# Three pairs by token halves instead of four, and twelve seven-block products ahead of the second projection, in layer 0 of a hybrid decoder trunk

## The chip, the cores and the metric

The kernel runs on one core of a Trainium2 chip. Its time is the device time of one execution in microseconds (us); the figure that counts is the median of several executions. A profile is one such execution, recorded by the hardware profiler. PE is TensorE, PEld its weight loads, DVE is VectorE, ACT is ScalarE, POOL is GpSimd, SP is SyncE, which here only issues DMAs.

## The reference

512 tokens of width 1024 go through two layers. Layer 0 is a causal convolution module and a SwiGLU feed-forward network (FFN); layer 1 is sliding-window attention over a shared K/V and a second FFN. The change touches layer 0 alone:

```python
# layer 0
h = h + conformer_conv(rmsnorm(h, norm_mix[0]), ...)   # pointwise + GLU, 31-tap depthwise conv,
                                                       # LayerNorm, swish, second pointwise ("pw2")
h = h + swiglu_ffn(rmsnorm(h, norm_ffn[0]), ffn_w_up[0], ffn_w_down[0])

def swiglu_ffn(x, w_up, w_down):                       # width 1024 -> 2 x 2816 -> 1024
    gate, up = jnp.split(x @ w_up, 2, axis=-1)
    return (jax.nn.silu(gate) * up) @ w_down
```

All values are float32.

## The kernel before

**Arithmetic.** Activations are kept transposed (channels on the 128 partitions, tokens along the row). Most float32 products are done in three passes: `mm3` splits weight and activation into a high and a low part of type float32r and adds high x high, high x low and low x high. Each weight chunk is 128x1024 floats (512 KB). SP loads it into a `raw` tile (six buffers); ACT casts it to `whi`, and DVE subtracts to get `wlo` (four buffers each). This is done three chunks ahead of TensorE (`SPLIT_AHEAD`), in the fixed order `PLAN`. A cast for chunk n can run only when the fourth chunk before it has left its `whi` buffer, that is, when TensorE has finished with it.

**Layer 0 by token halves.** The 512 tokens go through the convolution in two halves of 256 (`h0`, `h1`). The FFN's 2816 hidden channels are eleven pairs of 256. Pairs 0 to 3 (`HALVES0[0]`) are computed for each token half as soon as that half is there: up products, gate, down products. For the first half (`part 0`) each chunk is 24 matmuls with 256 columns (`mm3`; the second projection and pair 0 use unsplit float32); for the second half (`twin`, `mm2`) each chunk is 16 matmuls: high x (high and low side by side), 512 columns, and low x high, 256 columns.

**Layer 0 by seven products.** Pairs 4 to 10 are computed for all 512 tokens with a Winograd form of Strassen's scheme: weights and activations are cut into 2x2 blocks, and seven block products (`SEVEN`: A11, S1, S2, A12, S3, S4, A22, each against a block or a sum of blocks of x) replace eight. Each product is one chunk: 24 matmuls with 256 columns. The sums of weight blocks S1 to S4 are made in DRAM: SP copies a block, POOL issues a DMA that adds another onto it (`prepare`, one step for each `share` of a chunk). The sums of x, T1 to T4 (`Rows0.sums`), are made on DVE as a job that is spread over part 1. The products A12 of pairs 4, 5 and 6 (`FIRST`) need the first token half alone and stand before the second half's projection; ACT copies their results away.

**What sets the order.** `PLAN` sets the order of the chunks. `job(gen, *points)` spreads a generator's steps over the following chunks by hand-written points (chunk count, steps done). The second half's convolution (`second`: taps on DVE, POOL and ACT, then the LayerNorm statistics through TensorE, then the rows `z`) is such a job; a call of `flush` runs what is left. The framework's scheduler then orders each engine's instructions from the program, within what depends on what.

Per seven-product pair DVE and ACT bring the products from PSUM into a tile `c` (c11, c12, c21, c22), then `gates` multiplies by the norm's scale, applies SiLU on ACT, multiplies on POOL, and `split` writes the hidden rows (`hid0`) in high and low parts. After all seven pairs the down products (512 columns, 14 chunks of 24 matmuls) run, and attention follows.

The lines that the prediction speaks of: L380 to L382 are the three matmuls of `mm3`, L412 and L413 the two of `mm2`, L378 unsplit float32; L294 and L297 are the cast and the subtraction of a weight chunk, L261 its load, L289 the accumulating DMA of `prepare`; L1089 is the matmul that spreads the second half's LayerNorm scales, L1101 to L1103 and L544/L545 make the rows `z`; L1295 makes T1 to T4; L830 to L842 bring products from PSUM; L849, L850, L852 and L853 are `gates`. In the changed kernel the same lines stand a little lower (L294 becomes L297, L297 becomes L300, L1103 becomes L1124).

## Time and profile before

| what | value |
|---|---|
| median of three runs | 1044.91 us (1043.2 to 1046.06) |
| profiled execution | 1043.27 us, of which the span from first to last instruction is 1041.5 us |
| busy in the span | PE 1031.5 us, PEld 932.6, DVE 776.5, ACT 613.0, POOL 473.2 |
| granted TensorE clock | 0.997 |
| instructions | 17709 |

A row of a view of groups reads: line, engine, operation, tiles out<-in, shapes, count | busy us in all, mean ns of one | idle us before them and what ended it. A row of the timeline reads: start in us, duration, engine, line, operation, tiles, count. Matmuls overlap in the array, so their durations are longer than their distance from start to start, and it is that distance which adds up to time.

### The profile page before, as it was taken

The page shows a single profiled execution, that of the slowest core. Times are in us where ns is not written, and L with a number is a line of the kernel's source. Part 1 is how long each engine was busy: PE and PEld are TensorE (multiplying, and loading weights), DVE is VectorE, ACT ScalarE, POOL GpSimd, SP SyncE. Part 2 cuts the span into 40 slices and gives each one's busy share as a digit, 9 for nine tenths or more (in the row PEclk, how much of TensorE's full clock was granted, in tenths as well). Part 3 has the DMA queues.
Part 4 walks back from the last instruction along what each step waited for, and adds up shares of the span by engine and source line. Part 5 has one row for each costly group of instructions (what it writes and reads, how often), then busy time and mean ns, then how long its engine had stood idle before and what let it go on. Part 6 is the DMA issues. An engine that isn't in the chain of part 4 may idle for free.

```text
span 1041.5 us, 17709 instructions
## 1 busy us (share of the span) xinstructions
PE 1031.5 (99%) x6580; PEld 932.6 (90%) x6580; DVE 776.5 (75%) x1202; ACT 613.0 (59%) x1062; POOL 473.2 (45%) x569
## 2 busy tenths in 40 slices
PE   9999999999999999999999999999999999999996
PEld 8888889999988999998888877788989999898995
DVE  3999989978789777673536566678686877868777
ACT  3887798847776556552333565466655556554654
POOL 3999999930535233221214255405442334434134
PEclk9999999999999999999999999999999999999998
DMA  9999747999999988999969766955879988877742
GB/s 356 340 315 207 205 126 204 272 256 275 249 239 262 304 220 284 256 301 244 286 209 254 210 183 183 228 154 152 252 230 312 287 264 264 245 233 222 224 150 81
DMA packets 67282, 248.33 MB, mean 238 GB/s; under 512 B 7579, under 2 KB 13884, under 8 KB 66364
## 3 DMA queue, kind: packets, MB, share of 16 engines
q1 hardware_dynamic: 54236, 200.75, 55.9%
q0 software_dynamic: 12672, 46.14, 24.8%
q8 instruction: 51, 0.84, 0.3%
q10 hardware_dynamic: 288, 0.31, 0.1%
q14 instruction: 35, 0.29, 0.1%
HBM read 241.93 MB, written 97.52 MB: 326 GB/s over the span
## 4 chain that ended last, share of the span: by engine, by line
PE 98%; DMA 0%; DVE 0%; issue 0%; POOLq 0%; SPq 0%; POOL 0%; ACT 0%
PE bank L380 20%; PE bank L382 20%; PE bank L381 20%; PE bank L960 10%; PE bank L902 9%; PE bank L412 4%; PE bank L378 4%; PE bank L413 2%; PE bank L1441 1%; PE bank L1483 1%; PE bank L1470 1%; PE bank L1058 1%; PE bank L1607 1%; PE bank L948 1%; DMA both<-in_lead_dram 0%; PE bank L1562 0%
## 5 line engine op out<-in xcount | busy, mean ns | idle before, releaser
L297 DVE TENSOR_TENSOR wlo<-raw,whi 128x1024 fp32r<-128x1024 f32 x246 | 329.7, 1348 | 136.8 <-ACT whi L294 136.5
L294 ACT CAST whi<-raw 128x1024 fp32r<-128x1024 f32 x246 | 257.1, 1049 | 276.6 <-PE bank L381 194.1
L380 PE MATMUL bank<-quad,whi 128*128 128x256 f32 (+1 forms) x976 | 307.4, 317 | 0.0
L381 PE MATMUL bank<-quad,whi 128*128 128x256 f32 (+1 forms) x976 | 306.6, 315 | 0.0
L382 PE MATMUL bank<-quad,wlo 128*128 128x256 f32 (+1 forms) x976 | 305.7, 315 | 0.0
L380 PEld LDWEIGHTS bank<-quad,whi 128*128 128x128 f32 x976 | 185.5, 191 | 12.8 <-issue 1.6
L381 PEld LDWEIGHTS bank<-quad,whi 128*128 128x128 f32 x976 | 186.0, 191 | 11.9 <-issue 0.5
L382 PEld LDWEIGHTS bank<-quad,wlo 128*128 128x128 f32 x976 | 185.6, 191 | 11.8 <-issue 0.4
L853 POOL TENSOR_TENSOR up<-up 128x512 f32<-128x512 f32 x34 | 62.9, 1851 | 283.6 <-ACT up L850 283.6
L1002 POOL TENSOR_TENSOR pr<-pr,pr 128x256 f32<-128x256 f32 x208 | 155.4, 788 | 2.6 <-ACT pr L1001 2.5
L380 PE MATMUL bank<-rows,whi 128*128 128x256 f32 x488 | 138.0, 283 | 0.0
L381 PE MATMUL bank<-rows,whi 128*128 128x256 f32 x488 | 137.8, 282 | 0.0
L382 PE MATMUL bank<-rows,wlo 128*128 128x256 f32 x488 | 137.8, 282 | 0.0
L1009 DVE SCALAR_TENSOR_TENSOR bank<-apad,wdw,bank 128x256 f32<-128x256 f32 x248 | 112.4, 485 | 3.4
L1001 ACT ACTIVATE pr<-apad,wdw 128x256 f32<-128x256 f32 x208 | 98.3, 502 | 14.9 <-POOL pr L1002 13.1
L960 PE MATMUL bank<-quad,w 128*128 128x256 f32 x448 | 98.7, 380 | 0.0
L960 PEld LDWEIGHTS bank<-quad,w 128*128 128x128 f32 x448 | 84.9, 190 | 11.8 <-DVE bank L1009 0.2
L380 PEld LDWEIGHTS bank<-rows,whi 128*128 128x128 f32 x488 | 93.1, 191 | 0.3
L381 PEld LDWEIGHTS bank<-rows,whi 128*128 128x128 f32 x488 | 93.1, 191 | 0.3
L382 PEld LDWEIGHTS bank<-rows,wlo 128*128 128x128 f32 x488 | 93.0, 191 | 0.0
L491 POOL TENSOR_TENSOR tmp<-tmp,tmp 128x256 f32<-128x256 f32 (+1 forms) x28 | 26.8, 957 | 101.4 <-ACT tmp L487 96.2
L412 PE MATMUL bank<-quad,whi 128*128 128x512 f32 x168 | 59.7, 398 | 0.0
(230 smaller groups left out, 1635.9 us busy)
## 6 DMA issues: line engine op xcount, KB each, us to landing
raw<-in_W_dram SPq DMA_DIRECT2D x170, 512.0 KB, 5.7
raw<-sum SPq DMA_DIRECT2D x88, 512.0 KB, 5.4
sum<-in_W_dram SPq DMA_DIRECT2D x52, 512.0 KB, 6.2
sum<-in_W_dram POOLq DMA_DIRECT2D x44, 512.0 KB, 9.6
sum<-sum POOLq DMA_DIRECT2D x44, 512.0 KB, 8.5
sum<-in_W_dram SPq DMA_DIRECT2D x4, 3584.0 KB, 30.4
w<-in_W_dram SPq DMA_DIRECT2D x14, 512.0 KB, 8.6
sum<-in_W_dram SPq DMA_DIRECT2D x4, 1024.0 KB, 30.3
```

The costliest lines, as they stand in the source:

```text
L294: on_act = nc.scalar.copy(hi, src).ins
L297: latest[:] = [on_act, lo_engine[0].tensor_sub(lo, src, f32(hi)).ins]
L380: nc.tensor.matmul(out, w[0], x[0], start=start, stop=False, **kw)
L381: nc.tensor.matmul(out, w[0], x[1], start=False, stop=False, **kw)
L382: nc.tensor.matmul(out, w[1], x[0], start=False, stop=stop, **kw)
L412: nc.tensor.matmul(first[2], first[0], first[1], start=start, stop=False)
L853: pool_op(nc.gpsimd.tensor_mul(gate, gate, c[:, m, :, 1, :]))
L902: nc.tensor.matmul(out, x, w[:, ws], start=first and e == 0 and i == 0, stop=e == 1 and i == 2, skip_group_check=True)
L960: mm = nc.tensor.matmul(self.pb[:, w * W2:(w + 1) * W2], w1_of(ct, w, k), x[k] if x else xg[k][:, tok], start=k == 0, stop=k == KT - 1)
L1001: on_act = nc.scalar.mul(pr, a[:, j:j + W2], tap(j))
L1002: on_pool = pool_op(nc.gpsimd.tensor_add(pr, acc, pr))
L1009: on_dve = nc.vector.scalar_tensor_tensor(yt if i == nd - 1 else c, src, tap(i), c if i else self.shift, op0=ALU.mult, op1=ALU.add)
```

## The change

`HALVES0` puts three pairs instead of four through the token halves, so that eight pairs (3 to 10) go by seven products. Ahead of the second projection stand twelve products instead of three: A12 of all eight pairs and A11 of pairs 4 to 7; where a pair has both, A12 is added onto A11 in the same PSUM bank, and ACT copies both stages away. Part 2 is cut in two groups of four pairs (`GROUPS0`), each followed by its down products. The points of the second convolution's job reach over 50 counts instead of 35; those of the sums of x begin at count 10 instead of 11 and end at 27 instead of 32. The LayerNorm statistics are ordered behind the last matmul issued (`stamp`). The addition of the first half's FFN into `h` is put off into the early products (`let_go`). `share`, the sums of weights prepared for each chunk, is 0.5 instead of 0.45 in the halves and 0.45 instead of 0.25 in part 2. The tiles `c` of odd pairs move to another pool.

```diff
-HALVES0 = ((0, 4), (4, 11))
-FIRST = (4, 5, 6)
+HALVES0 = ((0, 3), (3, 11))
+GROUPS0 = ((3, 7), (7, 11))
+FIRST11 = (4, 5, 6, 7)
+FIRST = [(4, "A11"), (3, "A12"), (4, "A12"), (5, "A11"), (8, "A12"), (5, "A12"),
+         (6, "A11"), (9, "A12"), (6, "A12"), (7, "A11"), (10, "A12"), (7, "A12")]
...
-        if pair in FIRST:
-            names = ["A11", "S1", "S2", "S4", "S3", "A22"]
+        names = ["A11", "S1", "S2", "S4", "S3", "A22"][pair in FIRST11:]
         steps += [(pair, names[0])] + held
-        held = [(pair, names.pop())] if pair in FIRST else []
+        held = [(pair, names.pop())]
...
-    plan.extend(("up0", *step) for step in part2_products())
-    downs(*HALVES0[1])
+    for group in GROUPS0:
+        plan.extend(("up0", *step) for step in part2_products(group))
+        downs(*group)
...
             if a == "A11":
-                if self.early is None:
+                if "A12" in self.early:
+                    nc.vector.tensor_add(c11, r, self.early["A12"])
+                else:
                     nc.scalar.copy(c11, r)
...
+            elif a == "S1" and self.p1 is not None:
+                nc.scalar.copy(c11, self.early["A12"])
+                nc.vector.scalar_tensor_tensor(c22, r, -1.0, self.p1, op0=ALU.mult, op1=ALU.subtract)
             elif a == "S1":
                 nc.scalar.mul(c22, r, -1.0)
+            elif a == "S2" and self.p1 is not None:
+                nc.vector.tensor_add(c12, r, self.p1)
             elif a == "S2":
                 nc.scalar.copy(c12, r)
...
+            elif a == "A22" and self.p1 is not None:
+                nc.vector.scalar_tensor_tensor(c21, r, -1.0, self.p1, op0=ALU.mult, op1=ALU.subtract)
...
-        job(second, (base, 0), (base + 8, 19), (base + 13, 22), (base + 26, 40), (base + 30, 45), (base + 34, 50), (base + 35, h1.n_steps - early - 3))
+        job(second, (base, 0), (base + 8, 17), (base + 13, 20), (base + 26, 34), (base + 38, 40), (base + 41, 43), (base + 42, 44),
+            (base + 43, 44), (base + 44, 45), (base + 45, 46), (base + 47, 48), (base + 48, 49), (base + 50, h1.n_steps - early))
...
-        preparing[0], share[0] = prepare(), 0.45
+        preparing[0], share[0] = prepare(), 0.5
...
-        for pair in FIRST:
+        chains = {}
+        for n, (pair, a) in enumerate(FIRST):
             pace()
-            r = new_chain()
-            product(("up0", pair, "A12"), [[x0["ffn0"][4 + k][e][:, HALF[0]] for k in range(4)] for e in range(2)], r, True)
-            nc.scalar.copy(first[pair], r)
+            if n < 2:
+                let_go()
+            begins = pair not in chains
+            r = chains.setdefault(pair, new_chain() if begins else None)
+            j = 4 * (a == "A12")
+            product(("up0", pair, a), [[x0["ffn0"][j + k][e][:, HALF[0]] for k in range(4)] for e in range(2)], r, begins, pace)
+            nc.scalar.copy(first[pair][a], r)
         flush()
...
-    job(rows0.sums(), (base + 11, 0), (base + 19, 8), (base + 26, 14), (base + 32, 17))
+    job(rows0.sums(), (base + 10, 0), (base + 14, 8), (base + 17, 10), (base + 20, 12), (base + 23, 14), (base + 27, 17))
...
-    share[0] = 1 / 4
+    share[0] = 0.45
+    for group in GROUPS0:
...
         for g in range(2):
             banks = accs(512)
             down_group([(("down", 0, kp, g), 2 * (kp - lo0)) for kp in range(lo0, hi0)], lambda kt: hid0[kt], banks)
             for m in range(4):
                 nc.vector.tensor_add(h[g * 4 + m], banks[m], h[g * 4 + m])
-                nxt.on_h(g * 4 + m)
+                if last:
+                    nxt.on_h(g * 4 + m)
```

ACT, from the LayerNorm scales of the second half (L1085, in the changed kernel L1106) to the first two rows `z` (SiLU at L1103, now L1124, and their cast), before. whi504 belongs to the last early product, whi509 and whi517 to the first two chunks of the second projection, quad499 holds the high parts of `z`:

```order
L1085 ACTIVATE tmp493_2535<-ident_134,rr492_2533 128x128 x2
L294 CAST whi504_2615<-raw470_2383 128x1024
L294 CAST whi509_2653<-raw473_2413 128x1024
L294 CAST whi517_2710<-raw478_2449 128x1024
L1103 ACTIVATE tmp501_2605<-tmp501_2605,prm_76 128x256
L1103 ACTIVATE tmp506_2644<-tmp506_2644,prm_76 128x256
L544 CAST quad499_2603<-tmp501_2605 128x256
L544 CAST quad499_2603<-tmp506_2644 128x256
```

The same place now; whi521, whi532, whi541 and whi544 are the first four chunks of the second projection, bank519 is the product A12 of pair 10, the last but one ahead of it:

```order
L1106 ACTIVATE tmp514_2702<-ident_134,rr513_2700 128x128 x2
L297 CAST whi532_2811<-raw494_2556 128x1024
L1293 COPY quad461_2349<-bank515_2707 128x512
L297 CAST whi541_2867<-raw498_2588 128x1024
L1293 COPY c11465_2353<-bank519_2742 128x512
L1124 ACTIVATE tmp526_2765<-tmp526_2765,prm_76 128x256
L1124 ACTIVATE tmp527_2784<-tmp527_2784,prm_76 128x256
L549 CAST quad524_2763<-tmp526_2765 128x256
L549 CAST quad524_2763<-tmp527_2784 128x256
L297 CAST whi544_2898<-raw502_2620 128x1024
L1293 COPY c11462_2350<-bank515_2707 128x512
L1124 ACTIVATE tmp528_2790<-tmp528_2790,prm_76 128x256
```

The first SiLU stood behind the cast of the second projection's second chunk, and stands now behind that of its third and behind the copy of an early product.

DVE in part 2, from one pair's gates to the next, before (up701 is the tile `c` of pair 5):

```order
L840 TENSOR_TENSOR up701_3915<-bank711_3994,up701_3915 128x512
L849 TENSOR_TENSOR up701_3915<-up701_3915,rsbc292_1398 128x2x256
L852 TENSOR_TENSOR up701_3915<-up701_3915,rsbc292_1398 128x2x256
L297 TENSOR_TENSOR wlo728_4125<-raw703_3918,whi727_4124 128x1024
L838 TENSOR_TENSOR up701_3915<-up701_3915,bank702_3916 128x512
L297 TENSOR_TENSOR wlo731_4156<-raw706_3949,whi730_4155 128x1024
L545 TENSOR_TENSOR quad710_3989<-up701_3915,quad709_3988 128x512
L830 TENSOR_TENSOR up724_4120<-bank725_4121,quad497_2600 128x512
L297 TENSOR_TENSOR wlo735_4201<-raw712_3995,whi734_4200 128x1024
L297 TENSOR_TENSOR wlo738_4232<-raw715_4026,whi737_4231 128x1024
```

And now (up693 is that of pair 4, up717 that of pair 5):

```order
L845 SCALAR_TENSOR_TENSOR up717_4050<-bank718_4051,quad461_2349 128x512
L300 TENSOR_TENSOR wlo730_4134<-raw700_3908,whi729_4133 128x1024
L550 TENSOR_TENSOR quad704_3948<-up693_3871,quad703_3947 128x512
L859 SCALAR_TENSOR_TENSOR up693_3871<-bank705_3953,quad461_2349 128x512
L300 TENSOR_TENSOR wlo733_4166<-raw706_3954,whi732_4165 128x1024
L849 TENSOR_TENSOR up717_4050<-bank727_4130,quad461_2349 128x512
L868 TENSOR_TENSOR up693_3871<-up693_3871,rsbc292_1401 128x2x256
L871 TENSOR_TENSOR up693_3871<-up693_3871,rsbc292_1401 128x2x256
L300 TENSOR_TENSOR wlo736_4197<-raw711_3988,whi735_4196 128x1024
L857 TENSOR_TENSOR up717_4050<-bank718_4051,up717_4050 128x512
```

Between two weight subtractions there stood one other instruction or two, or none; now there stand two or three.

More of the change, by code (lines that the diff above doesn't have):

```diff
@@ L583, in down_group, with let_go @@
                 on_step()
+    held = []
+    def let_go():
+        b, rs_bc, into = held.pop(0)
+        nc.vector.tensor_mul(b, b, rs_bc)
+        nc.vector.tensor_add(into, b, into)
     def ffn_part(layer, part, xg, tok, rms, on_h=None, twin=False, plain=None):
@@ L619, in ffn_part @@
                 for e, b in enumerate(full):
-                    i = g * 4 + 2 * e
-                    nc.vector.tensor_mul(b, b, rs_bc)
-                    nc.vector.tensor_add(hT[:, i:i + 2, tok], b, hT[:, i:i + 2, tok])
-                    for k in range(2 if on_h is not None else 0):
-                        on_h(i + k)
+                    into = hT[:, g * 4 + 2 * e:g * 4 + 2 * e + 2, tok]
+                    held.append((b, rs_bc, into))
                 continue
@@ L799, in hybrid_trunk, with product @@
     PARTNER = dict(n.split() for n in SEVEN)
-    def product(key, block, r, opens, closes=True):
+    def product(key, block, r, opens, between=None):
         w = [x.rearrange("p (a k c) -> p a k c", a=2, k=4) for x in get_seven(*key)]
         for which in range(2):
+            if which and between is not None:
+                between()
             for k in range(4):
@@ L812, in hybrid_trunk, with __init__ @@
     class SevenPair:
-        def __init__(self, kind, pair, rows, c, c11=None):
-            self.kind, self.pair, self.rows, self.c, self.early = kind, pair, rows, c, c11
+        def __init__(self, kind, pair, rows, c, early=None):
+            self.kind, self.pair, self.rows, self.c, self.early = kind, pair, rows, c, early or {}
+            self.p1 = self.early.get("A11")
             self.chains = {}
@@ L1132, in background @@
                 yield
-                self.spread()
+                with tc.issue_after(stamp[0]):
+                    self.spread()
                 yield from self.rows(True)
```

100 lines of the change are left out of this document (58 added, 42 removed).

## The prediction

> **What bounds the kernel now.** I read the page first, its busy times, its slices and the chain that ended last.
>
> ```profile
> span 1041.5 us, 17709 instructions
> PE 1031.5 (99%) x6580; PEld 932.6 (90%) x6580; DVE 776.5 (75%) x1202; ACT 613.0 (59%) x1062; POOL 473.2 (45%) x569
> DVE  3999989978789777673536566678686877868777
> PE 98%; DMA 0%; DVE 0%; issue 0%; POOLq 0%; SPq 0%; POOL 0%; ACT 0%
> ```
>
> TensorE is busy from end to end and 98% of the last chain is its own. A busy PE need not be at its peak, so the list of its waits comes next.
>
> ```profile
> PE bank L465 <- POOL ones_m L462: 1.1, 1, 1.1
> PE bank L948 <- DVE quad L922: 0.7, 2, 0.4
> ```
>
> Those are all of them, 1.8 us, and both lie at the start. So in layer 0 every change counts by the distance from one matmul's start to the next, and by any wait that appears where there was none. For the distances I took unbroken stretches of the timeline; each two rows are the first and the last of one.
>
> ```profile
> 182.22 0.28 PE L380 MATMUL bank<-quad,whi 128*128 128x256 f32 x1
> 194.93 0.28 PE L381 MATMUL bank<-quad,whi 128*128 128x256 f32 x1
> ...
> 327.48 0.40 PE L412 MATMUL bank<-quad,whi 128*128 128x512 f32 x1
> 332.42 0.40 PE L412 MATMUL bank<-quad,whi 128*128 128x512 f32 x1
> ...
> 335.21 0.28 PE L380 MATMUL bank<-quad,whi 128*128 128x256 f32 x1
> 339.62 0.28 PE L381 MATMUL bank<-rows,whi 128*128 128x256 f32 x1
> ...
> 473.12 0.40 PE L380 MATMUL bank<-quad,whi 128*128 128x512 f32 x1
> 478.36 0.39 PE L382 MATMUL bank<-quad,wlo 128*128 128x512 f32 x1
> ```
>
> In the first half 12.71 us hold 106 distances: 119.9 ns for 256 columns. In the second half 4.94 us hold 14 pairs (512 and 256 columns): 352.9 ns. In the seven products 4.41 us hold 37: 119.2 ns, or 2.86 us a product. In the down products 5.24 us hold 23: 227.8 ns for 512 columns, or 5.47 us a chunk.
>
> **The matmuls that go and come.** Pair 3 leaves the halves. In the first half it had four up and two down chunks of 24: 144 x 119.9 = 17.27 us. In the second it had six chunks of eight such pairs of matmuls: 48 x 352.9 = 16.94 us. It comes back as seven products, 168 x 119.2 = 20.03 us, and two down chunks, 48 x 227.8 = 10.93 us. 34.21 less 30.96: 3.25 us are saved. The nine further early products and the second group of down products only move. The Trainium skill ("TensorE: Matmul & The Clock Gate", Wait — 56ns, not 53.3ns?) gives a warm start-to-start distance of columns / 2.4 GHz plus about 2.5 ns, so 109.2 ns for 256 columns; as the 512-column matmuls are equally many before and after (48), it would save 24 x 109.2 = 2.62 us, an estimate from that page. The rows above show 119 to 120 ns, and two prices for 512 columns, so the measurement decides.
>
> **The second projection.** Its activations `z` come from a chain behind the spread of the LayerNorm scales (L1089): DVE, ACT, DVE. These rows show ACT and DVE there.
>
> ```profile
> 234.44 0.86 PE bank L1089 x2
> ...
> 238.08 1.05 ACT L294 CAST whi<-raw 128x1024 fp32r<-128x1024 f32 x1 [2.63 <-PE bank L381]
> 239.04 1.09 ACT L1103 ACTIVATE tmp<-tmp,prm 128x256 f32<-128x256 f32 x2
> 240.03 0.70 ACT L544 CAST quad<-tmp 128x256 fp32r<-128x256 f32 x2
> 240.64 0.57 ACT L1257 COPY quad<-bank 128x512 f32<-128x512 f32 x1
> ...
> 240.99 0.76 DVE L545 TENSOR_TENSOR quad<-tmp,quad 128x256 fp32r<-128x256 f32 x2
> ```
>
> The first SiLU stands in ACT's queue behind a weight cast that waits until TensorE gives up its buffer, at 238.1. From there to the first low part of `z` it takes until 240.99 + 0.4, some 3.3 us. After the spread come three products, so the projection begins at 235.3 + 8.6 = 243.9, and 2.5 us were to spare. Now the SiLU stands one cast later, behind that of the third chunk, which waits for the end of the last product but one; one product, 2.86 us, is left, and a copy of 0.57 us stands between. The first low part is then there 3.3 + 0.5 = 3.8 us after the release, 0.9 us late, of which 0.1 us is covered by the first matmul. The third and fourth rows stand in the same way behind the next cast, one copy and three SiLUs of some 0.5 us, and are some 0.3 us late again. I take 1.0 us; the ends are 0 (a shorter chain) and one product, 2.86 us (one cast more in the way). Whatever else of the wider convolution moves here is DVE work that the longer stretch makes room for: DVE shows 9 in six of its second to eighth slices, and the convolution now has twelve products beside it. A11 and A12 are plain blocks of the weights, so the early products wait for no sum from POOL's queue, which the convolution fills there. The copies of the early products, twelve instead of three on ACT, cost nothing as long as the chain above is not lengthened.
>
> **The sums of x and the first group.** These windows and groups bear on DVE.
>
> ```profile
> 300.00:320.00 20.00, 20.00 (x115) 17.35 (x114) 19.84 (x20) 14.16 (x21) 8.95 (x7) 1.00 0.84 252
> 320.00:340.00 20.00, 20.00 (x129) 18.05 (x128) 19.80 (x28) 11.33 (x18) 9.84 (x13) 1.00 1.01 255
> ...
> L297 DVE TENSOR_TENSOR wlo<-raw,whi 128x1024 fp32r<-128x1024 f32 x107 | 144.8, 1359 | 47.0 <-ACT whi L294 46.8
> L849 DVE TENSOR_TENSOR up<-up,rsbc 128x512 f32<-128x512 f32 x14 | 9.6, 686 | 0.1
> L545 DVE TENSOR_TENSOR quad<-up,quad 128x512 fp32r<-128x512 f32 x13 | 8.9, 683 | 1.8 <-ACT quad L544 1.8
> L853 POOL TENSOR_TENSOR up<-up 128x512 f32<-128x512 f32 x14 | 26.9, 1924 | 102.0 <-ACT up L850 102.0
> L289 POOL DMA_DIRECT2D sum<-in_W_dram x23 | 21.3, 1015 | 0.0
> ...
> L297 DVE TENSOR_TENSOR wlo<-raw,whi x62: 1209/1226/3446, 169.7 to 349.1; 128x1024 fp32r<-128x1024 f32 x62
> ```
>
> From 300 to 340, with the sums of x, DVE was busy for 39.6 of 40 us, and TensorE still did not wait: weights are split three products (8.6 us) ahead. The sums stay as dense (13 counts), and now a tighter stretch follows at once. Pair 5 cost DVE nine instructions of some 0.69 us and six subtractions of 1.36, 14.3 us, beside six products, 17.2 us. With A11 and A12 taken early it has eleven and five: 7.6 + 6.8 = 14.4 us beside five products, 14.3 us. So for pairs 4 to 6 DVE has no slack. I take 0.5 us, as the lead has held; the ends are 0 and 3 us, a third of the 8.6. The subtraction takes 1.36 us on average; of the 62 in the last row the shortest took 1.21 and the longest 3.45, and no row says what held that one. The Trainium skill ("SBUF — State Buffer", SBUF: two separate sides) says that VectorE with two SBUF inputs and GpSimd lock the same pair of ports, and that the loser waits for the whole instruction. By it all POOL work of the group, eight gate multiplies and ten DMA issues, could fall on DVE, and the sum would be no gain; the mean row speaks for a small part of it, and the rest is the second rival.
>
> **Edits at nothing, with their cover.** The first group's last pair: its A22 now stands behind a down chunk and a quarter, and its hidden rows are needed by the fourth, 1.75 chunks or 9.6 us later. Before, the last A22 ended at 473.1, where the 512-column stretch quoted above begins, and the rows were there at 480.80, 7.7 us later (first row below):
>
> ```profile
> 480.11 0.69 DVE L545 TENSOR_TENSOR quad<-up,quad 128x512 fp32r<-128x512 f32 x1
> ...
> 480.00:540.00 60.00, 60.00 (x266) 49.69 (x265) 21.75 (x22) 16.28 (x19) 9.42 (x13) 1.00 0.88 253
> ```
>
> So 1.9 us are to spare; with the cover gone it costs up to 1.5 us, at both groups' ends. The second set of down groups adds eight additions into `h` on DVE, 5.5 us at 0.69, but among down chunks DVE works for 21.75 of 60 us (second row). The put-off additions (`let_go`) and the stamped statistics move by a product or two on queues that now have more products beside them. Three loads and three splits fewer cost nothing, since nobody waits for them.
>
> **The sum.** -3.25 + 1.0 + 0.5 = -1.75 us. Against the profiled execution, 1043.27 us (span 1041.5 and 1.8 around it), that is 1041.5. The median of the runs, 1044.91, lies 1.64 above that execution, and on its scale I predict 1043.2 us, 0.17% less. About 0.3% (3.1 us) is what a measurement of this kernel can tell from no change.
>
> **The rivals.** First, both covers hold and the whole 3.25 us show: 1041.7 us. For it speaks that TensorE waited nowhere beyond the start; against it that the ACT queue's rows leave less time than they need. Chance 0.25, and half of that falls past the 0.3%.
>
> Second, slower: DVE becomes the bound of the first group. Its POOL work is 8 x 1.92 + 10 x 1.02 = 25.6 us; if half of it blocks DVE, 12.8 us, less the 3.0 that the mean subtraction already holds (20 x 0.15 over the least, 1.21), 9.8 us are added. It decides from where the lead is used up: with 6.3 us of lead (8.6 less a cast and a subtraction) TensorE stands 3.5 us, 1046.2; with none, as 39.6 of 40 suggest, 9.8 us, 1052.5. Chance 0.15, above 1048 for 0.09 of it.
>
> Third, also slower: the DMA queues. These rows cover 320 us.
>
> ```profile
> q1 hardware_dynamic: 16244, 63.23, 54.9%
> q0 software_dynamic: 5482, 19.97, 35.5%
> raw<-in_W_dram SPq DMA_DIRECT2D x82, 512.0 KB, 6.7
> raw<-sum SPq DMA_DIRECT2D x28, 512.0 KB, 5.9
> sum<-in_W_dram POOLq DMA_DIRECT2D x23, 512.0 KB, 9.1
> sum<-sum POOLq DMA_DIRECT2D x19, 512.0 KB, 9.3
> sum<-in_W_dram SPq DMA_DIRECT2D x10, 512.0 KB, 7.4
> ...
> DMA to landing us min/median/max: 3.3/7.4/13.9
> ```
>
> A load or copy costs 175.7 / 120 = 1.46 us of all engines, an accumulation (42 of them) 2.70. With 0.45 sums a chunk, each copied and accumulated, a product asks for 1.46 + 0.45 x 4.16 = 3.33 us in 2.86; with 0.25 it was 2.50. Over 21 and 23 products that lacks 9.9 and 10.8 us, and the down chunks between make it good. A chunk is asked for six products before its split, 17.2 us, less 7.4 to land: 9.8 us of cover, about enough. With landings of 10.6, half-way to the longest, the cover is 6.6 us, and 3.3 and 4.2 us show: 1043.2 + 7.5 = 1050.7. The Trainium skill ("DMA: Bandwidth & Descriptors", Queues, rings and completion order) says that each engine goes round-robin between its queues by packets, so that accumulations would take their turn from the loads. No run here shows that yet; DMA shares of 1.01 without a PE wait speak against it. Chance 0.10.
>
> The change may also do a bit less than it says, with a stall of a product at the projection and 1.5 us at each group's end: -3.25 + 2.86 + 0.5 + 3.0 = +3.1 at most, 1046 in the middle, chance 0.08. The forecast keeps 0.42.
>
> **The numbers.** The time is the forecast's own, 1043.2 us. Faster by over 0.3% (below 1041.8): half of the first rival and a quarter of the forecast, by the scatter of the runs (1.7 and 1.2 us about their median): 0.24. Slower (above 1048.0): 0.09 of the second rival, the third, and 0.01 of the fourth: 0.20. Within: 0.56. The forecast's own range, with its two unknown waits between none and twice what I take, is 1041.7 to 1044.7. The range for 8 in 10 runs from 1040.6, the whole saving and 1 us of scatter, below which lies 0.05, to 1049.5, above which lies the upper half of the second and third rival, 0.13.
>
> **What would show it.** In the changed profile PE holds 24 matmuls less; its waits, or its distances, show about 1 us at the first chunks of the second projection, with ACT's SiLU behind a cast that waits for PE; the first group shows DVE near 100% and TensorE's distances still 119 ns. It is wrong if the distances stretch over many products of a group: with DVE at 100% that is the second rival, with ACT casts waiting for DMA it is the third.

## The result, and the profile after

The changed kernel takes 1047.97 us (median of seven executions) where the kernel before takes 1044.91 (also of seven). Six of the seven lie at 1047.72 to 1049.71; the other, at a granted clock of 0.654, took 1459.69 and is not in the ratio. The ratio, taken over the executions and not from the two medians, is 1.0033, 95% interval 1.0023 to 1.0044: slower by some 3.4 us, just past the 0.3% (3.1 us) that the prediction took as the least to be told from no change. The profiled execution after has a span of 1046.2 us (before 1041.5), of which 1.2 us is a longer wait at the start (L969 below, L948 before). That wait changes from one profile to the next, from 0.2 to 1.9 us over the profiles of this document, and I put it down to the execution and not to layer 0's order.

The page of the changed kernel, its first lines and the chain that ended last; then its whole list of TensorE's waits (us in all, times, longest):

```profile
span 1046.2 us, 17673 instructions
PE 1030.7 (99%) x6556; PEld 929.7 (89%) x6556; DVE 789.0 (75%) x1216; ACT 607.8 (58%) x1055; POOL 478.6 (46%) x573
PE 93%; DVE 4%; issue 1%; DMA 1%; ACT 0%; POOL 0%; POOLq 0%; SPq 0%; DVEq 0%; ACTq 0%
```

```profile
PE bank L385 <- DVE up L840: 2.8, 1, 2.8
PE bank L969 <- DVE quad L941: 1.9, 2, 1.6
PE bank L470 <- POOL ones_m L467: 1.1, 1, 1.1
PE bank L418 <- DVE wlo L300: 0.8, 2, 0.6
PE bank L386 <- DVE quad L550: 0.6, 2, 0.4
PE bank L385 <- ACT quad L1293: 0.2, 1, 0.2
```

6580 matmuls have become 6556, the 24 that the prediction took out. TensorE's share of the last chain has gone from 98% to 93%, and DVE's from 0% to 4%: there are now waits in layer 0, and nearly all are for DVE. The second and third row are the start; the others are new. The longest is one single wait, of the first matmul of pair 3's S2, for the addition at L840. Below are the timelines of TensorE and DVE in the changed kernel, then the same addition and the same place in the kernel before, where it is pair 4's:

```profile
337.40 0.28 PE L387 MATMUL bank<-rows,wlo 128*128 128x256 f32 x1
340.44 0.36 PE L385 MATMUL bank<-rows,whi 128*128 128x256 f32 x1 [2.77 <-DVE up L840]
...
339.62 0.68 DVE L840 TENSOR_TENSOR up<-bank,quad 128x512 f32<-128x512 f32 x1
```

```profile
339.93 0.68 DVE L830 TENSOR_TENSOR up<-bank,quad 128x512 f32<-128x512 f32 x1
...
340.81 0.28 PE L382 MATMUL bank<-rows,wlo 128*128 128x256 f32 x1
340.93 0.28 PE L380 MATMUL bank<-rows,whi 128*128 128x256 f32 x1
```

These rows hold most of the answer. The pair's A11 and S2 accumulate in one bank, and S2 may begin only when the addition of the early A12 has read A11. DVE gets to that addition at 339.6 us now and at 339.9 us before, practically the same moment. TensorE came for the bank at 340.93 before, 0.3 us after it was free; now it comes at 337.5 and stands. The chunks that TensorE was spared brought it here sooner, and DVE did not come along. The windows of both kernels (length, busy PE, PEld, DVE, ACT, POOL with instructions, granted clock, DMA share, GB/s), the first two rows after, the last two before, show why:

```profile
299.00:320.00 21.00, 21.00 (x120) 18.13 (x118) 21.00 (x22) 13.70 (x22) 10.91 (x9) 1.00 0.94 208
330.00:344.00 14.00, 11.23 (x90) 10.84 (x89) 13.38 (x21) 6.58 (x11) 11.06 (x13) 1.00 0.88 240
```

```profile
299.00:320.00 21.00, 21.00 (x122) 18.23 (x121) 20.27 (x21) 15.16 (x22) 9.23 (x7) 1.00 0.85 253
330.00:344.00 14.00, 14.00 (x105) 13.31 (x105) 13.29 (x18) 6.86 (x11) 8.16 (x10) 1.00 1.04 278
```

DVE is full in both, TensorE waits only after. Part 1 is six chunks of 2.82 us (16.9 us) shorter, but of DVE's work only pair 3's went, some 10.5 us (six subtractions at 1.36, four additions at 0.41, one low part at 0.69); the sums of x and the updates of `h` stayed whole. The waits for DVE's low parts of weights (L300) at 319 to 324 us lie in the same full stretch; the experiments show that they come with the sooner sums of x.

To see all of it I added up, from the timeline, every distance between two matmul starts that is over 90 ns longer than usual for its kind (120 ns for 256 columns, 228 or 235 ns for 512; 216 ns for 256 columns of unsplit float32), by how much it is longer. The matmuls that the scales and statistics put in between are counted too, alike in every column. In us:

| stretch (us) | before | after | A11 by ACT | points as before | both | both, z sooner | small POOL ops |
|---|---|---|---|---|---|---|---|
| 40 to 186 | 1.1 | 1.5 | 1.9 | 1.6 | 1.7 | 1.7 | 1.7 |
| 186 to 262 | 0.8 | 3.3 | 3.3 | 3.3 | 3.3 | 2.7 | 3.4 |
| 262 to 300 | 0.2 | 0.2 | 0.2 | 0.2 | 0.2 | 0.2 | 0.2 |
| 300 to 332 | 0 | 1.4 | 1.4 | 0 | 0 | 0 | 0 |
| 332 to 400 | 0 | 2.9 | 0.8 | 2.4 | 0.2 | 0.2 | 0 |
| 400 to 640 | 1.9 | 1.6 | 1.9 | 1.7 | 1.8 | 1.8 | 1.8 |
| sum | 4.0 | 10.9 | 9.5 | 9.3 | 7.3 | 6.6 | 7.1 |
| sum less 4.0 less the 3.25 saved | | +3.7 | +2.3 | +2.1 | +0.1 | -0.6 | -0.1 |
| measured, (ratio - 1) x 1044 | | +3.4 | +1.3 | +1.8 | +0.3 | -0.8 | -0.5 |

The last five columns are experiments, below. The saving of 3.25 us, taken as the prediction had it, and the waits together give the measured difference within 0.4 us but for one (1.0 us), where the interval of the ratio is 0.9 us to either side.

### The profile page after: what moved, and what is told of

Read it like the earlier page. It is cut to its first block, busy times and chain, and to the rows that moved or that the text cites. A ratio compares the mean times of both kernels' runs of the same rounds, so it can differ in the third digit from the quotient of the medians.

```text
span 1046.2 us, 17673 instructions
## 1 busy us (share of the span) xinstructions
PE 1030.7 (99%) x6556; PEld 929.7 (89%) x6556; DVE 789.0 (75%) x1216; ACT 607.8 (58%) x1055; POOL 478.6 (46%) x573
## 4 chain that ended last, share of the span: by engine, by line
PE 93%; DVE 4%; issue 1%; DMA 1%; ACT 0%; POOL 0%; POOLq 0%; SPq 0%; DVEq 0%; ACTq 0%
PE bank L385 20%; PE bank L386 20%; PE bank L387 20%; PE bank L981 10%; PE bank L921 9%; PE bank L383 4%; PE bank L417 2%; DVE wlo L300 1%; PE bank L1485 1%; PE bank L1527 1%; PE bank L1514 1%; PE bank L418 1%; PE bank L1079 1%; PE bank L1651 1%; DMA both<-in_lead_dram 1%
## 5 line engine op out<-in xcount | busy, mean ns | idle before, releaser
L297 ACT CAST whi<-raw 128x1024 fp32r<-128x1024 f32 x243 | 253.7, 1049 | 275.4 <-PE bank L386 194.7
L300 DVE TENSOR_TENSOR wlo<-raw,whi 128x1024 fp32r<-128x1024 f32 x243 | 319.5, 1321 | 120.0 <-ACT whi L297 115.2
L872 POOL TENSOR_TENSOR up<-up 128x512 f32<-128x512 f32 x36 | 67.1, 1863 | 314.7 <-ACT up L869 305.6
L385 PE MATMUL bank<-rows,whi 128*128 128x256 f32 x512 | 144.6, 283 | 2.8 <-DVE up L840 2.8
L386 PE MATMUL bank<-rows,whi 128*128 128x256 f32 x512 | 144.6, 282 | 0.0
L387 PE MATMUL bank<-rows,wlo 128*128 128x256 f32 x512 | 144.5, 283 | 0.0
L385 PEld LDWEIGHTS bank<-rows,whi 128*128 128x128 f32 x512 | 97.5, 191 | 3.3 <-issue 2.9
L386 PEld LDWEIGHTS bank<-rows,whi 128*128 128x128 f32 x512 | 97.6, 191 | 0.3
L387 PEld LDWEIGHTS bank<-rows,wlo 128*128 128x128 f32 x512 | 97.5, 191 | 0.0
L921 PE MATMUL bank<-wlo,fhi 128*128 128x512 f32 x140 | 55.2, 394 | 0.0
```

Of the source, the lines that this page charges most:

```text
L297: on_act = nc.scalar.copy(hi, src).ins
L300: latest[:] = [on_act, lo_engine[0].tensor_sub(lo, src, f32(hi)).ins]
L385: nc.tensor.matmul(out, w[0], x[0], start=start, stop=False, **kw)
L386: nc.tensor.matmul(out, w[0], x[1], start=False, stop=False, **kw)
L387: stamp[0] = nc.tensor.matmul(out, w[1], x[0], start=False, stop=stop, **kw).ins
L872: pool_op(nc.gpsimd.tensor_mul(gate, gate, c[:, m, :, 1, :]))
```

## The experiments

My theory after the result: DVE is late from 299 to 343 us, and of its late instructions one holds a bank. Rivals: the waits only move when one is taken away; the sums of x as such; GpSimd and its transfers. Each run was taken beside the kernel before, whose median was then 1044.04, 1043.44 or 1043.71 us, and its ratio is to those executions: compare ratios, not times.

**ACT frees the bank.**

```diff
-                    nc.vector.tensor_add(c11, r, self.early["A12"])
+                    nc.scalar.copy(c11, r)
+                    nc.vector.tensor_add(c11, c11, self.early["A12"])
```

> The changed kernel with one edit: pair 3's A11 (the one product that is added to an early A12) is first copied out of its bank by ACT, and DVE adds the early part SBUF to SBUF afterwards. DVE keeps as many additions. Theory (DVE is late from 299 to 343 us, and one of its late instructions, the addition that frees the bank at 339.6, holds TensorE for 2.8 us): that one wait goes, about 2.5 us come back, so about 0.5 us over the time before (ratio 1.000 to 1.001) instead of 3.1; no wait on that bank in the list of waits. Rival A (queues or the raised share of prepared sums slow everything a little): nothing changes, ratio 1.003. Rival B (DVE's lateness only moves): the 2.8 us come back as waits for low parts of weights within the next products, ratio 1.002 to 1.003.

Measured: 1045.47 us, ratio 1.0012 (1.0003 to 1.0021). The bank's wait is gone from the list of TensorE's waits; one of 0.6 us for a low part has come at 343 us:

```profile
PE bank L387 <- DVE wlo L300: 0.6, 1, 0.6
```

The theory holds for most of it, and the rival that waits move for a quarter: 2.9 us became 0.8.

**The last step of the updates of `h` on GpSimd.**

```diff
-                    nc.vector.tensor_add(hm, hm, t)
+                    pool_op(nc.gpsimd.tensor_add(hm, hm, t))
```

> The changed kernel with one edit: the last step of the second half's updates of h (eight additions of 128x256 for each part-1 group pair, 4.4 us of DVE between 329 and 343) runs on GpSimd instead of DVE. Theory (DVE's lateness): the addition that frees pair 3's bank comes some 3 us sooner, so the 2.8 us wait shrinks to under 0.5 us and the ratio to 1.000 to 1.001; the waits at 319 to 324 us (1.4 us) stay. Rival (GpSimd and DVE hold each other up at the SBUF, so work moved from DVE to GpSimd costs DVE as much): subtractions of 1.2 us stretch to 1.7 and more beside the eight additions, the wait stays over 2 us, ratio 1.003 or more.

Measured: 1047.95 us, ratio 1.0038 (1.0026 to 1.0051), no better than the changed kernel. 4.6 us went off DVE, but the last five subtractions of weights before 345 us took 1.58 to 1.79 us instead of 1.21 to 1.68, and a wait of 1.9 us was left at the same matmul. TensorE's clock was halved for 3.4 us after it (last section), which took 1.4 us more. Here the rival was right: work moved from DVE to GpSimd is paid for in part by DVE. Another part went into hand-overs: ACT's copies at L616 waited 3.5 us for GpSimd's additions (2.2 us for DVE's in the changed kernel), DVE stood idle for 1.6 us behind ACT, and the addition at L840 began at 339.1 us, only 0.5 us sooner.

**The sums of x at the points of the kernel before**, and **three counts sooner still.**

```diff
-    job(rows0.sums(), (base + 10, 0), (base + 14, 8), (base + 17, 10), (base + 20, 12), (base + 23, 14), (base + 27, 17))
+    job(rows0.sums(), (base + 11, 0), (base + 19, 8), (base + 26, 14), (base + 32, 17))
```

> The changed kernel with the sums of x (T1 to T4) at the points of the kernel before (base+11 to base+32 in place of base+10 to base+27). Theory (DVE has one amount of work for 299 to 343 us and no room): the waits at 319 to 324 us go, since T2's and T3's work comes later, but the same work then stands between the h updates and the first products, so the wait at 337 us stays or grows and others join it: ratio 1.002 to 1.006. Rival (it is the sooner sums as such that cost): back to the saving without its loss, 4 us less, ratio 0.999.

```diff
-    job(rows0.sums(), (base + 10, 0), (base + 14, 8), (base + 17, 10), (base + 20, 12), (base + 23, 14), (base + 27, 17))
+    job(rows0.sums(), (base + 10, 0), (base + 12, 8), (base + 14, 10), (base + 17, 12), (base + 20, 14), (base + 24, 17))
```

> The changed kernel with the sums of x three counts sooner still (base+10, +12, +14, +17, +20, +24 for its steps 0, 8, 10, 12, 14, 17). Theory (DVE's lateness at 299 to 343 us, after 6.6 us of idle time on DVE between 287 and 299): about 3 us of T1's work slides into that idle time and the rest of it stands clear of the h updates; the waits at 319 to 340 us (4.3 us) fall to 1 to 2, ratio 0.9995 to 1.001. Rival (the sums are not the cause; the updates of h and their hand-over between DVE and GpSimd alone make the addition late): the wait at 337 us stays at 2.5 us or more, ratio 1.002 to 1.003. If the sooner T1 instead delays the low parts of weights at 300 us, the waits move there and the ratio stays at 1.003.

Measured: as before 1045.9 us, ratio 1.0017 (1.0008 to 1.0026); sooner 1049.74 us, ratio 1.0054 (1.0041 to 1.0067). With the points of before the waits at 319 to 324 us went, as the theory had it, but the loss at 332 to 400 us shrank, from 2.9 to 2.4 us, where I had it stay or grow. I missed the second run altogether. List of TensorE's waits with the sooner sums:

```profile
PE bank L417 <- DVE tmp L654: 1.8, 1, 1.8
PE bank L385 <- DVE up L840: 1.5, 1, 1.5
```

DVE's idle time from 285 to 345 us was 7.0 us, against 7.1 in the changed kernel: the sums did not slide into it. In the changed kernel the idle time lies in front of instructions that wait, 4.2 of the 7.1 us in front of subtractions that wait for ACT's cast. The sums stood ahead of the additions that empty part 1's banks (L654) instead. So sooner is worse and later is better: the sums should stand as late as their products allow. In the run with the points of before, the scheduler also put S4 ahead of S2, whose T2 is there later, and so the bank's wait fell behind another product.

**The sooner sums alone, on the kernel before** (24 chunks in part 1).

> The kernel before with one part of the change alone: the sums of x at the changed kernel's points (base+10 to base+27), with 24 chunks in part 1 as before. Theory (DVE has 17 us more of part 1 here for 10 us more of work, so sooner sums find some room, but DVE had no idle time from 300 to 343 us): 0 to 1 us of waits, ratio 1.000 to 1.001. Rival (it is the sooner sums as such that cost, the shorter part 1 does not matter): 2 us of waits for low parts of weights, ratio 1.002 or more.

Measured: 1045.08 us, ratio 1.0017 (1.0007 to 1.0026). One wait stands there, and nothing at a bank:

```profile
PE bank L413 <- DVE wlo L297: 1.5, 1, 1.5
```

So the sooner points cost 1.8 us of long distances by themselves, at 320 to 324 us, more than I had given them and nearer to the rival. With the points of before (the run above) the changed kernel still loses 2.4 us at 332 to 400 us. Together that is 4.2 us, and the changed kernel lost 4.3. That the 2.4 us come from the shorter part 1 is argued from the windows; no run gave part 1 its six chunks back.

**GpSimd's multiplications of part 1 left out.**

```diff
-                nc.gpsimd.tensor_mul(t1v, t1v, rs_bc.unsqueeze(1).to_broadcast([P, 2, w]))
...
-                pool_op(nc.gpsimd.tensor_mul(t2, t1, t2))
...
-                    pool_op(nc.gpsimd.tensor_mul(t, t, rs_bc))
```

> The changed kernel without GpSimd's three multiplications of part 1 (left out of the computation: the scaling of the first up half and the gate product for each pair, and the scaling in the updates of h; so the second half's share of the output lacks them). DVE, ACT and TensorE keep every instruction and their order. Theory (GpSimd's operations hold DVE: single DVE operations between 285 and 345 us stand at 1.66 to 3.04 us where their like take 1.21, 8.2 us in all, and that is the whole lateness): all DVE operations of 128x1024 take 1.21 to 1.25 us there, the waits at 319 to 340 us (4.3 us) fall under 1 us, ratio 0.9985 to 1.000. Rival (it is the number of DVE instructions in a part 1 that is one pair shorter, and the long ones are long for another reason): the long ones stay, the waits stay over 3 us, ratio 1.002 to 1.003. Since the rows of part 1 are also ready sooner without the multiplications, only the durations and DVE's own idle time tell the two apart for certain.

Measured: 1048.98 us, ratio 1.005 (1.0038 to 1.0063). The durations came out as the theory has it: all twenty subtractions 1.21 to 1.23 us, DVE's operations from 285 to 345 us 49.0 us in all instead of 56.7, and no wait at 319 to 324. But the wait at the bank grew to 3.5 us with DVE idle for 12.7 us in that stretch. ACT and DVE there:

```profile
336.01 1.05 ACT L297 CAST whi<-raw 128x1024 fp32r<-128x1024 f32 x1 [1.73 <-DMA raw<-sum]
...
337.09 1.23 DVE L300 TENSOR_TENSOR wlo<-raw,whi 128x1024 fp32r<-128x1024 f32 x1 [0.65 <-ACT whi L297]
338.23 1.09 DVE L618 TENSOR_TENSOR h<-h,tmp 128x256 f32<-128x256 f32 x3
339.24 0.68 DVE L837 TENSOR_TENSOR up<-bank,quad 128x512 f32<-128x512 f32 x1
```

The addition stands behind a subtraction, that behind a cast, and that behind a load. With the multiplications gone, GpSimd issued its accumulating transfers earlier, and the loads of sums took 13.5 us to land in place of 8.9:

```profile
raw<-sum SPq DMA_DIRECT2D x9, 512.0 KB, 13.5
```

```profile
raw<-sum SPq DMA_DIRECT2D x9, 512.0 KB, 8.9
```

(DMA issues from 300 to 345 us, without the multiplications and in the changed kernel; the last column is the median from issue to landing.) So this run changed two things. I repeated it with GpSimd's instructions kept and cut to 8 or 16 columns; one of the three edits:

```diff
-                    pool_op(nc.gpsimd.tensor_mul(t, t, rs_bc))
+                    pool_op(nc.gpsimd.tensor_mul(t[:, 0:16], t[:, 0:16], rs_bc[:, 0:16]))
```

> The changed kernel with GpSimd's three multiplications of part 1 cut to 8 or 16 of their columns (so the second half's share of the output is not scaled and gated but for these), in place of leaving them out: GpSimd keeps every instruction, so the accumulating transfers that it issues stay in their order behind them; without them these had run ahead, and loads landed after 13.5 us instead of 8.9. Theory (GpSimd holds DVE by up to 1.8 us an operation): DVE's operations of 128x1024 at 1.21 to 1.25 us, DVE some 7 us less busy between 285 and 345, no wait at 319 to 324, and the wait at pair 3's bank under 1 us since its addition no longer comes late; ratio 0.9995 to 1.001. Rival (the addition stands behind updates of h and a subtraction whose cast waits for a load, so DVE's load does not matter to it): the bank wait stays at 2 us or more with DVE idle ahead of it; ratio 1.002 or more.

Measured: 1043.15 us, ratio 0.9995 (0.9986 to 1.0004), as the theory had it. Its group of subtractions from 298 to 343 us, and that of the changed kernel:

```profile
L300 DVE TENSOR_TENSOR wlo<-raw,whi 128x1024 fp32r<-128x1024 f32 x16 | 19.5, 1222 | 4.2 <-ACT whi L297 4.2
```

```profile
L300 DVE TENSOR_TENSOR wlo<-raw,whi 128x1024 fp32r<-128x1024 f32 x16 | 22.5, 1408 | 1.3 <-ACT whi L297 1.3
```

With DVE undisturbed there is no wait over 0.1 us from 300 to 400 us, and some 4 us are back. The scheduler placed a few of DVE's instructions differently here, and GpSimd's short operations also hand their results over sooner, so I take it as a strong sign, not as a price of the disturbance alone.

**Fewer prepared sums of weights**: `share` 0.45 in place of 0.5 in the halves, 0.35 in place of 0.45 in the groups.

> The changed kernel with fewer sums of weights prepared per chunk: 0.45 in place of 0.5 in the first half, 0.35 in place of 0.45 in the groups of four pairs (0.25, the value before, doesn't prepare them in time). Theory (DVE's lateness, not the DMA queues): no change beyond 0.5 us, the same waits at the same places, ratio 1.0025 to 1.004. Rival (the accumulating transfers take turns with the loads and slow TensorE a little everywhere, and GpSimd's queue of transfers holds up its multiplications): 1.5 to 3 us less, ratio 1.0005 to 1.002.

Measured: 1048.3 us, ratio 1.0045 (1.0033 to 1.0058); the waits of the changed kernel at 319 to 340 us stayed (1.4 and 2.9 us of long distances), and new ones of 2.0 and 0.9 us for low parts came at 213 and 222 us. Fewer sums are no cure; the raised shares are not the cause of the waits at 319 to 340 us.

**The second convolution's end two counts sooner.**

```diff
-        ... (base + 26, 34), (base + 38, 40), (base + 41, 43), ... (base + 50, h1.n_steps - early))
+        ... (base + 24, 34), (base + 36, 40), (base + 39, 43), ... (base + 48, h1.n_steps - early))
```

> The changed kernel with the end of the second convolution's background work (its statistics, scales, spread and z) two counts, one product, sooner. Theory (the second projection stands 1.3 us for z because ACT's first SiLU comes behind a cast that waits for TensorE): one product, 2.86 us, more room, so the 1.3 us at 254 to 259 us fall under 0.4 us and the rest stays; ratio 1.0015 to 1.0025 against 1.0033. Rival (z is late because DVE and ACT are full there, not because of where it was put): the waits stay at 1 us or more, or the convolution that is now pressed into two counts less stops the products at 204 to 232 us; ratio 1.003 or more.

Measured: 1050.45 us, ratio 1.006 (1.0046 to 1.0074). The waits at the second projection did go (1.4 us to none), but the taps, pressed together, stopped TensorE at 199 to 224 us for 2.2 us more, as the rival had it. The rest of the loss is in the last section.

**Together.** With both edits of the bank and of the points, and z as just above:

> The changed kernel with three edits together: ACT copies pair 3's A11 out of its bank and DVE adds the early part afterwards; the sums of x stand at the points of the kernel before; the second convolution's end stands two counts sooner. Theory (the saving of 3.25 us is real, and the loss is made of separate waits: 1.3 us at the second projection, 1.4 at the weights' low parts at 319 to 324, 2.9 at pair 3's bank, 1.1 at three other places): the first three fall to 1.5 us together, the rest stays; 3.25 less 2.6 is some 0.7 us less than before, ratio 0.9985 to 1.0000. Rival (DVE has one amount of work for this stretch, and waits only move): 1 to 2 us of waits come back between 335 and 370, ratio 1.0005 to 1.002.

Measured: 1044.83 us, ratio 1.0013 (1.0004 to 1.0022). That is the rival's ratio, but not for its reason: from 295 to 400 us nothing over 0.2 us is left, and most of what remains is at 199 to 224. With bank and points alone:

> The changed kernel with two edits: ACT copies pair 3's A11 out of its bank (as in the first experiment) and the sums of x stand at the points of the kernel before. What the earlier runs showed: each edit alone gave back some 2 us and left 0.8 to 2.0 us of waits at 335 to 363 us; with a third edit the stretch from 295 to 370 us had no wait at all. Theory (two separate causes in that stretch, the bank that only DVE can free and the sums put too close): no wait over 0.2 us between 295 and 400 us, the waits of the first half and of the second projection (2.7 us over their usual distances) stay, 3.25 less 2.7 less some start-up: ratio 0.9985 to 1.0000. Rival (waits only move, DVE has one amount of work): 1 us or more comes back at 335 to 400, ratio 1.0005 to 1.002.

Measured: 1043.96 us, ratio 1.0003 (0.9994 to 1.0012), between the two forecasts; the trace is the theory's, with 0.2 us left from 300 to 400 us. So the 4.3 us of the stretch are accounted for by the bank and the points. And with only the spread of the scales and the rows of z one count sooner:

```diff
-(base + 45, 46), (base + 47, 48), (base + 48, 49), (base + 50, h1.n_steps - early))
+(base + 45, 46), (base + 46, 48), (base + 47, 49), (base + 49, h1.n_steps - early))
```

> As the run beside it (bank and points), and of the second convolution only the last two steps, the spread of its scales and the rows of z, one count (half a product) sooner; its taps stay where they are, since pressing them into two counts less moved the loss to 199 to 224 us. Theory (z is late by ACT's queue: the first SiLU then comes ahead of the cast it stood behind): the 1.3 us at the second projection fall under 0.4, no new wait at 199 to 232; ratio 0.9975 to 0.9990. Rival (z is late by DVE, which has subtractions of weights between its steps): at least 0.9 us stay, ratio like that of the run beside it.

Measured: 1043.21 us, ratio 0.9992 (0.9983 to 1.0001): the lowest ratio of all, 0.4% below the changed kernel and level with the kernel before or a little under it. ACT at the first rows of z, in the changed kernel and in this one:

```profile
251.79 1.05 ACT L297 CAST whi<-raw 128x1024 fp32r<-128x1024 f32 x1 [2.19 <-issue]
252.75 0.58 ACT L1293 COPY c<-bank 128x512 f32<-128x512 f32 x1
253.22 1.10 ACT L1124 ACTIVATE tmp<-tmp,prm 128x256 f32<-128x256 f32 x2
```

```profile
251.11 0.60 ACT L1125 ACTIVATE tmp<-tmp,prm 128x256 f32<-128x256 f32 x1 [1.32 <-DVE tmp L1124]
251.98 1.05 ACT L297 CAST whi<-raw 128x1024 fp32r<-128x1024 f32 x1 [0.27 <-PE bank L386]
```

The first SiLU now runs ahead of the cast, as meant, at 251.1 instead of 253.2; the second still stands behind it. Somewhat under half of the 1.4 us came back (3.3 to 2.7 us in the table), less than the theory had.

## Why the prediction was wrong

**The matmuls that go and come: right.** 24 fewer are in the trace, and with 3.25 us the table above closes.

**The second projection, 1.0 us: right in place and cause, a little small.** The first SiLU stands behind the third chunk's cast and the copy, as worked out. The distances from 254 to 259 us are 1.4 us too long. That the sum came so near is partly luck: 0.5 us stand at the first chunk, for which I had 0.8, and 0.9 at the second, for which I had 0.3.

**The sums of x and the first group, 0.5 us with ends 0 and 3: the step that failed.** It measured 4.3 us (1.4 at 319 to 324 and 2.9 at 337). That DVE was full from 300 to 340 us was read correctly; "as the lead has held" was the error. The lead had held against a part 1 of 24 chunks and sums of x that began later: they are as dense as before, as the prediction says (13 counts), but stand five counts sooner, and that alone cost the kernel before 1.8 us. I costed DVE's work against TensorE's for pairs 4 to 6, where it fits with room:

```profile
344.00:386.90 42.90, 42.90 (x363) 42.90 (x362) 36.24 (x44) 23.71 (x31) 12.70 (x9) 1.00 1.02 311
```

In three pairs' time (fifteen products) DVE is busy for 36.2 of 42.9 us, with 44 instructions; I had taken 43.2 us and 48. I did not cost it for part 1, which loses 16.9 us of TensorE and 10.5 us of DVE, so that a stretch already at 39.6 of 40 us is asked for 6.4 us more. And I did not ask what DVE holds besides the weights' low parts: the three chunks of lead protect those, but nothing in the program protects a PSUM bank that only an addition on DVE frees. Pair 4's addition had been there before, with 0.3 us to spare; no row of mine looked at it.

**The sum of edits at nothing: mostly right.** The two group boundaries and the eight extra additions cost nothing (400 to 640 us: 1.6 us of long distances after, 1.9 before). But 1.2 us that I had at nothing, since the longer stretch was to make room for the convolution's work on DVE, came in the first half: 0.7 around 203.8 us, at the low part of a hidden row that stands on DVE among the convolution's taps, and 0.4 at 232 us. Another 0.4 before 186 us I did not follow up.

**The rivals.** The second one, DVE as the bound, is nearest to what happened: its mechanism (GpSimd holding DVE's operations) is at work, and the time lies between its two prices, nearer the lower (1046.2; measured 1047.97). But it happened at the end of part 1 and the entry into pair 3, not over pairs 4 to 6, and the transfers that GpSimd issues, which the rival counted in, hold nothing (last section). I gave it 0.15. The third, the DMA queues, did not occur with this change: no cast or subtraction of the changed kernel waits for a DMA from 186 to 400 us. The run without the multiplications, where casts wait for loads for 12.1 us there, shows that it can be brought about. The first, both covers hold, was refuted. My own sign that the prediction is wrong, distances stretched over many products of a group, did not appear: it went wrong by single waits.

## What to carry to other kernels

A stretch that is made shorter for the bounding engine has to be costed for every engine that is full in it: take what leaves each, and compare it with what leaves the stretch. Look then for the instruction of the full engine that frees a bank or buffer, not just for the queue that has a lead, and give such a release to an engine with room (here ACT, 2 us for one copy). Work that is issued sooner need not fill an engine's idle time (DVE's stayed at 7 us here); it can stand ahead of what others wait for.

## What was not expected of the hardware

**GpSimd holds DVE where both of DVE's inputs lie in SBUF.** The changed kernel's DVE and GpSimd:

```profile
316.70 2.30 DVE L1331 TENSOR_TENSOR plain<-plain 128x1024 f32<-128x1024 f32 x1
325.83 1.21 DVE L1331 TENSOR_TENSOR plain<-plain 128x1024 f32<-128x1024 f32 x1
...
315.73 2.19 POOL L656 TENSOR_TENSOR tmp<-tmp,rsbc 128x512 f32<-128x512 f32 x1 [4.21 <-DVE tmp L654]
```

The same operation takes 1.21 us alone; begun at 316.70 beside a GpSimd operation that ends at 317.92, it takes the 1.22 us that are left of that, and about its own time. Additions with one input in PSUM (L654, L617) took 0.41 to 0.43 us throughout. From 285 to 345 us the prolongations come to 7.7 us (56.7 less 49.0). GpSimd's issues of transfers do not do this: in the same stretch the four subtractions that overlap such issues alone took 1.21 to 1.23 us. One of them begins amid two:

```profile
340.55 1.21 DVE L300 TENSOR_TENSOR wlo<-raw,whi 128x1024 fp32r<-128x1024 f32 x1
...
340.23 1.66 POOL L292 DMA_DIRECT2D sum<-in_W_dram  x2
```

The Trainium skill ("SBUF — State Buffer", SBUF: two separate sides) says so of two SBUF inputs against a GpSimd operation, and the trace agrees. The prolongations were there before the change too (six subtractions of 1.76 to 2.32 us from 285 to 345 us), but TensorE did not wait then.

**A wait of two microseconds can halve TensorE's clock for 3.4 or 6.8 more.** After the wait at pair 3's bank, with z two counts sooner (the first row is the wait's end), then the window of that run and that of the changed kernel (the 1.00 and 0.50 are the granted clock):

```profile
340.63 0.55 PE L385 MATMUL bank<-rows,whi 128*128 128x256 f32 x1 [2.78 <-DVE up L840]
340.98 0.42 PE L386 MATMUL bank<-rows,whi 128*128 128x256 f32 x1
341.20 0.41 PE L387 MATMUL bank<-rows,wlo 128*128 128x256 f32 x1
```

```profile
341.00:346.00 5.00, 5.00 (x25) 5.00 (x25) 2.76 (x4) 0.08 (x1) 1.95 (x3) 0.50 1.05 315
```

```profile
341.00:346.00 5.00, 5.00 (x44) 5.00 (x43) 3.80 (x5) 1.53 (x2) 1.75 (x3) 1.00 1.04 309
```

The same wait left the clock at 1.00 in one profile and at 0.50 in the other, where 26 distances of 213 ns instead of 120 cost another 2.4 us. In this way a part of the losses of four experiments (updates on GpSimd, sums sooner, multiplications left out, z two counts sooner) comes from the clock, after waits of 1.8 to 3.5 us. The executions of z two counts sooner show it too: two at a granted clock of 0.998 took 1048.03 and 1048.95 us, three at 0.994 to 0.996 took 1050.45 to 1051.53.

It goes with where the wait falls. In all fourteen profiles every change of the clock lies a whole number of steps of 3.41 us behind its first rise, which is 4 to 7 us into the span. Windows on that grid, z two counts sooner and then the changed kernel:

```profile
336.41:339.82 3.41, 1.45 (x13) 1.24 (x11) 3.41 (x7) 2.11 (x3) 3.31 (x4) 1.00 1.05 239
339.82:343.24 3.42, 2.61 (x12) 2.64 (x13) 3.42 (x7) 0.00 (x0) 3.13 (x4) 0.50 1.00 260
```

```profile
335.53:338.95 3.42, 2.15 (x19) 1.94 (x17) 3.42 (x7) 2.56 (x4) 2.63 (x3) 1.00 0.97 210
338.95:342.36 3.41, 1.92 (x16) 1.95 (x17) 3.41 (x6) 0.23 (x1) 3.41 (x5) 1.00 1.01 235
```

With z sooner TensorE stands for 1.96 us within one step (3.41 less its 1.45 of busy time), and the next step is halved, here with the one behind it; in the changed kernel the border of two steps cuts the same wait into 1.27 and 1.49 us, and nothing happens. In the profiles of this document, behind the start, each of the four steps with 1.88 to 2.42 us of waits was followed by a halved one, and no step at the full clock with up to 1.52 us was; what lies between, no run here shows. The Trainium skill ("TensorE: Matmul & The Clock Gate", The HAM clock gate) gives a free-running window of about 3.4 us and half the clock after an idle one. The steps of 3.41 us agree with it, but here a window that was idle for 1.88 us was enough (updates on GpSimd).
